# A conv feed-forward in two phases: the up projection first, its products in DRAM, then a down projection that accumulates its whole contraction in PSUM

## The chip, the core and the metric

The kernel runs on one core of a Trainium2 chip. A core has a matrix engine (TensorE, "PE" in the profile, with its weight loads as "PEld"), a vector engine (DVE), a scalar engine (ACT), a third elementwise engine (POOL) and a sync engine (SP). Each takes its own instructions in the order of its own queue; semaphores make one engine wait for another. Matrix products land in PSUM, which is used here as eight banks of 128 x 512 float32 values; everything else is worked on in SBUF. DMA transfers between SBUF and DRAM are issued from the queues of SP, POOL or ACT.

The metric is the device time of one execution in microseconds (us), lower is better.

## The reference, cut to what matters

One decoder layer (512 tokens, model width 2048) is computed: a modulated norm, two attention mixers, an output projection with residual, and then the feed-forward, which alone is changed here:

```python
D_MODEL, SEQ, D_FF, CONV_W = 2048, 512, 5632, 3

def conv_ffn(h, w_up, w_conv, b_conv, w_down):
    S = h.shape[1]
    u = h @ w_up                                   # (512, 2048) @ (2048, 11264)
    up = jnp.pad(u, ((0, 0), (CONV_W - 1, 0), (0, 0)))
    conv = b_conv
    for j in range(CONV_W):
        conv = conv + w_conv[j] * up[:, j:j + S]
    gate, val = jnp.split(conv, 2, axis=-1)
    return (jax.nn.silu(gate) * val) @ w_down      # (512, 5632) @ (5632, 2048)

h = rms_norm(x, g_ffn[l]) * (1.0 + sc_f) + sh_f
x = x + gt_f * conv_ffn(h, w_up[l], w_conv[l], b_conv[l], w_down[l])
```

All inputs and the output are float32.

## The kernel before

**Products of float32.** Every large product is made from three passes. A float32 operand is split into a high part (rounded by ACT to the type float32r) and a low remainder (DVE: operand minus high part). `mm3` (line 120) then issues three matmuls into the same bank: high x high, high x low, low x high (lines 121, 122, 123). `split` (line 116) does this for an activation tile of 128 x 512.

**Storage.** SBUF has 75 equal slots of 128 x 512 (`get`, `getr` for the type float32r, `put` to give back), handed out first in, first out. Weights go through `wtile` (line 97): SP loads 128 x 1024 values into one of five raw buffers, ACT makes the high part (line 110) in one of three buffers, DVE the remainder (line 111) in one of three. `wtile` runs at raised priority, so the scheduler puts the weights of later steps ahead of other work in the queues of SP, ACT and DVE.

**Who decides the order.** The program text is not the order of the queues: a scheduler with its own estimate of durations places the instructions of each engine; buffers and data dependences bind it.

**Up projection.** `lin_fm` (line 125) computes four 128-row tiles of the transposed result: stationary operand the weights, moving operand the activations `h2` (16 pairs of slots, high and low). One step takes two of the 16 tiles of the contraction and issues 24 matmuls into four banks. A block of 512 columns is eight steps.

**The loop.** `NG` = 11 groups of 512 feed-forward columns. Each group (lines 1126 to 1162) runs one up block for the gate columns and one for the value columns, on alternate halves of the PSUM banks (`half`, line 155). `conv` (line 1083) takes a finished bank through one ACT pass with bias and scale (line 1085) and two DVE passes that add the shifted rows (lines 1086, 1087). The gate tile goes through SiLU on ACT; `ev_v` multiplies value by gate (line 1144), splits the product and keeps the four pairs as `fs`.

**Down projection.** `down` (line 1093) runs one group behind: after the up blocks of a group the previous group's `fs` is multiplied with its 512 rows of `w_down`, for four blocks of 512 output columns. `lin_tm` (line 140) does this: stationary operand the activations, moving operand the weights, two contraction tiles a step, four token tiles in four banks, so that each bank takes six matmuls in a row. The sum over the 11 groups is kept in 16 SBUF slots `acc_f`: group 0 copies the banks there (ACT, line 1108), groups 1 to 9 add them (DVE, line 1118), and for group 10 the accumulators are first multiplied by the gate row `gf` (line 1101) and added to the residual `x1`, loaded from DRAM (lines 1100, 1102); each bank is then multiplied by `gf` (line 1113), added to that (line 1114) and stored by SP (line 1115).

**Beside it.** The rest of the adaLN modulation is computed in the gaps of the up blocks: a `ticker` calls `ada_stream` once in four steps, which loads 512 KB into a raw buffer and runs two DVE operations (lines 721, 723). `flush_cols` (line 747) sums such a block through two matmuls into a bank (lines 752, 753), and DVE adds a bias (line 757) that POOL has loaded (line 756).

Of the kernel before, what the change touches and what calls it, by code (L numbers as in the profile page):

```python
# [10 lines left out]
F32 = mybir.dt.float32  # L11
# [3 lines left out]
AF = mybir.ActivationFunctionType  # L15
ALU = mybir.AluOpType
AX = mybir.AxisListType

P = 128
T = 512  # L20
# [11 lines left out]
def trunk_layer_kernel(  # L32
# [28 lines left out]

# [1 line left out]
    cur = [None] * n_slots  # L63
# [3 lines left out]
    def get(dt=F32):  # L67
        i = free.popleft()
        if cur[i] is None or cur[i].dtype != dt:
            cur[i] = pool.tile([P, T], dt, name=f"slot{i}", tag=f"slot{i}")  # L70
        held[id(cur[i])] = i
        return cur[i]

    def getr():
        return get(F32R)

    def put(*ts):
        for t in ts:
            free.append(held.pop(id(t)))
# [36 lines left out]
    def split(dst_hi, dst_lo, src):  # L116
        A.activation(dst_hi, src, AF.Copy)  # L117
        V.tensor_tensor(dst_lo, src, r32(dst_hi), ALU.subtract)

    def mm3(o, lh, ll, rh, rl, first, last):  # L120
        PE.matmul(o, lh, rh, start=first, stop=False)  # L121
        PE.matmul(o, lh, rl, start=False, stop=False)  # L122
        PE.matmul(o, ll, rh, start=False, stop=last)  # L123
# [16 lines left out]
    def lin_tm(src, c0, n, act, K, banks, evac, k0=0, tick=None):  # L140
        for kg in range(0, K, 2):
            wh, wl = wtile(src, k0 + kg, 2, c0, n)
            for tb in range(4):
                ts = slice(tb * P, (tb + 1) * P)
                for i in range(2):
                    k = kg + i
                    ah, al = act[k]
                    mm3(banks[tb][:, :n], ah[:, ts], al[:, ts], wh[:, i, :], wl[:, i, :],
                        k == 0, k == K - 1)
                if kg + 2 == K:  # L150
                    evac(tb, banks[tb][:, :n])
            if tick:
                tick()

    def half():
        cnt["half"] += 1
        return bank[4:8] if cnt["half"] % 2 == 0 else bank[0:4]

# [1 line left out]
    ident = pool.tile([P, P], F32, name="ident")  # L160
# [49 lines left out]
    A.activation(c_act, bank[7][:, 0:16], AF.Silu)  # L210
    # causal bias: zeros, then the triangle of the diagonal block
    zslot = get()
# [9 lines left out]

# [1 line left out]
    ssx = pool.tile([P, 16], F32, name="ssx")  # L224
# [41 lines left out]

# [1 line left out]
    mod = pool.tile([P, 96], F32, name="mod")  # L268
# [43 lines left out]

    # input projection in quarters of the contraction: A = indexer, B = sparse k/v and part of the gates
    part = {"A": [get() for _ in range(7)], "B": [get() for _ in range(7)]}
# [101 lines left out]

# [1 line left out]
    pos_f = gslot[0:4, 384:384 + P]  # L418
# [77 lines left out]

# [1 line left out]
    kit = part["A"][6]  # L498
# [77 lines left out]

# [1 line left out]
    sq = [get(), get()]  # L578
# [51 lines left out]

# [1 line left out]
    att = {}  # L632
# [71 lines left out]

# [1 line left out]
    ada_blocks = [8, 9, 10, 11, 16, 17, 18, 19, 12, 13, 14, 15, 20, 21, 22, 23]  # L706
# [68 lines left out]

# [1 line left out]
    gate_d = [dram.tile([P, T], F32, name=f"gate{k}") for k in range(2 * KD)]  # L777
# [21 lines left out]

# [1 line left out]
    krot = pool.tile([P, 4, 64], F32, name="krot")  # L801
# [42 lines left out]

# [1 line left out]
    pairs = {}  # L846
# [96 lines left out]

    # first branch projection, kept in DRAM
    pa_d = [dram.tile([P, T], F32, name=f"pa{k}") for k in range(KD)]
# [28 lines left out]

# [1 line left out]
    ob = reload(ob_d) + [tuple(att["o"][0:2]), tuple(att["o"][2:4])]  # L976
# [34 lines left out]

# [1 line left out]
    ss1 = pool.tile([P, 16], F32, name="ss1x")  # L1013
# [66 lines left out]

# [1 line left out]

# [6 lines left out]

    acc_f = [[None] * 4 for _ in range(4)]  # L1090
    gf = []

    def down(grp, fs):
        last = grp == NG - 1
        for db in range(4):
            if last:
                for tb in range(4):
                    t = acc_f[tb][db]
                    xt = get()
                    G.dma_start(xt, x1_d[db][tb])  # L1100
                    V.tensor_tensor(t, t, gf[db], ALU.mult)
                    V.tensor_tensor(t, t, xt, ALU.add)
                    put(xt)

            def ev(tb, b, db=db):
                if grp == 0:
                    acc_f[tb][db] = t = get()
                    A.activation(t, b, AF.Copy)
                    return
                t = acc_f[tb][db]  # L1110
                if last:
                    o = get()
                    V.tensor_tensor(o, b, gf[db], ALU.mult)  # L1113
                    V.tensor_tensor(o, o, t, ALU.add)  # L1114
                    SP.dma_start(out[tb * P:(tb + 1) * P, db * 512:(db + 1) * 512], o)
                    put(o)
                else:
                    V.tensor_tensor(t, t, b, ALU.add)  # L1118

            lin_tm(w_down, db * 512, 512, fs, 4, half(), ev, k0=grp * 4)  # L1120
        for t in fs:
            put(*t)

    prev = None
    NG = DFF // 512
    for grp in range(NG):
        gt = []
        if grp == NG - 2:
            while next(stream, 0) is None:
                pass  # L1130

        def ev_g(m, b, grp=grp):
            t = conv(grp * 4 + m, b)
            A.activation(t, t, AF.Silu)
            gt.append(t)

        bk = half()
        flush_cols(bk[3])
        lin_fm(w_up, grp * 512, h2, KD, bk, ev_g, tick=ticker(TF))
        fs = []  # L1140

        def ev_v(m, b, grp=grp):
            t = conv(44 + grp * 4 + m, b)
            V.tensor_tensor(t, t, gt[m], ALU.mult)
            hi, lo = getr(), getr()
            split(hi, lo, t)
            put(t, gt[m])
            fs.append((hi, lo))

        bk = half()  # L1150
        flush_cols(bk[3])
        lin_fm(w_up, DFF + grp * 512, h2, KD, bk, ev_v, tick=ticker(TF))
        if grp == NG - 1:
            for t in h2:
                put(*t)
            put(*ada_acc)
            for db in range(4):
                gf.append(get())
                G.dma_start(gf[db], gtr_d[20 + db])
        if prev is not None:  # L1160
            down(*prev)
        prev = (grp, fs)
    down(*prev)

# [25 lines left out]
```

## Time and profile before

| | us |
|---|---|
| median of 3 runs | 2795.78 (2795.48 to 2797.96) |
| span of the profiled execution, first to last instruction | 2791.8 |
| TensorE busy in it | 2753.4 |
| start of the first up matmul (L121) | 1314.29 |
| start of the last down matmul (L123) | 2786.91 |
| end of the last DVE operation | 2788.75 |

How to read the profile's rows: a busy row gives the busy time of each engine, its share of the span and the number of instructions. A window row gives the stretch in us, its length, and then, for PE, PEld, DVE, ACT and POOL, busy us and the number of instructions; at its end stand the granted TensorE clock (1.00 is full), the busy share of the 16 DMA engines and GB/s. A group row gives line, engine, operation, output <- inputs, shape and count, then busy us and mean ns of one, then the engine's idle time before these instructions and what ended it. A timeline row gives start, duration, engine, line and operation; in brackets the idle time before it. A DMA row gives the count, the size of one and the median time from issue to landing. Matmuls are pipelined: one lasts about 0.39 us, but the next starts 0.23 us after it.

### The profile page before, as it was taken

What the parts mean: (1) busy time and instruction counts of PE and PEld (TensorE: products, weight loads), DVE (VectorE), ACT (ScalarE), POOL (GpSimd) and SP (SyncE); (2) the same over time, 40 slices, a digit from 0 to 9 for tenths busy, and PEclk for the clock granted to TensorE, in tenths of its full rate; (3) what the DMA queues carried; (4) which work ended last, traced back from release to release, by engine and by line L of the source; (5) the groups of instructions that cost most, each with busy time, mean ns of one, the idle gap of its engine ahead of it and who ended that gap; (6) DMA issues with size and microseconds to landing.
All of it is one profiled execution on the core that took longest, in us unless ns stands there. A gap on an engine that the chain in (4) does not pass through costs nothing.

```text
span 2791.8 us, 31818 instructions
## 1 busy us (share of the span) xinstructions
PE 2753.4 (99%) x12160; PEld 2204.5 (79%) x12160; DVE 1550.7 (56%) x2615; ACT 903.2 (32%) x1309; POOL 177.5 (6%) x355
## 2 busy tenths in 40 slices
PE   6999999999999999999999999999999999999999
PEld 5877777788887768887888888888888888888887
DVE  7987975544467658546444353635263544434357
ACT  4333433322344553224333222222223231313231
POOL 1000100100031231000000000000000000000010
PEclk8999999999999999999999999999999999999999
DMA  9942245655464587645333433334343333333352
GB/s 321 362 138 87 68 138 176 203 188 174 151 204 132 161 293 255 207 153 186 91 98 103 123 106 113 121 106 122 98 129 98 114 98 99 97 92 98 97 168 98
DMA packets 222604, 409.43 MB, mean 147 GB/s; under 512 B 16714, under 2 KB 58084, under 8 KB 222452
## 3 DMA queue, kind: packets, MB, share of 16 engines
q1 hardware_dynamic: 200628, 348.59, 40.0%
q0 software_dynamic: 21792, 58.81, 6.2%
q8 instruction: 95, 1.56, 0.2%
q14 instruction: 57, 0.47, 0.1%
q10 hardware_dynamic: 32, 0.01, 0.0%
HBM read 376.93 MB, written 30.41 MB: 146 GB/s over the span
## 4 chain that ended last, share of the span: by engine, by line
PE 53%; DVE 0%; ACT 0%; issue 0%
PE bank L121 18%; PE bank L123 17%; PE bank L122 17%; DVE slot L1114 0%; DVE slot L1113 0%; PE bank L240 0%; ACT slot L1043 0%; PE bank L752 0%; PE bank L753 0%; ACT slot L1075 0%; PE bank L1041 0%
## 5 line engine op out<-in xcount | busy, mean ns | idle before, releaser
L111 DVE TENSOR_TENSOR wlo<-raw,whi 128x1024 fp32r<-128x1024 f32 (+2 forms) x462 | 558.2, 1209 | 868.6 <-ACT whi L110 865.6
L110 ACT ACTIVATE whi<-raw 128x1024 fp32r<-128x1024 f32 (+2 forms) x462 | 483.8, 1049 | 1418.4 <-PE bank L122 755.7
L121 PE MATMUL bank<-slot,whi 128*128 128x512 f32 (+1 forms) x2192 | 868.4, 398 | 2.7 <-ACT slot L1075 1.5
L122 PE MATMUL bank<-slot,whi 128*128 128x512 f32 (+1 forms) x2192 | 866.3, 395 | 0.0
L123 PE MATMUL bank<-slot,wlo 128*128 128x512 f32 (+1 forms) x2192 | 861.7, 396 | 0.0
L121 PE MATMUL bank<-whi,slot 128*128 128x512 f32 (+2 forms) x1472 | 572.1, 392 | 7.2 <-ACT slot L384 6.5
L122 PE MATMUL bank<-wlo,slot 128*128 128x512 f32 (+2 forms) x1472 | 575.6, 391 | 0.0
L123 PE MATMUL bank<-whi,slot 128*128 128x512 f32 (+2 forms) x1472 | 566.1, 389 | 0.0
L123 PEld LDWEIGHTS bank<-slot,wlo 128*128 128x128 f32 (+1 forms) x2192 | 411.0, 188 | 99.4 <-issue 1.9
L121 PEld LDWEIGHTS bank<-slot,whi 128*128 128x128 f32 (+1 forms) x2192 | 410.7, 187 | 98.7 <-ACT whi L110 2.1
L122 PEld LDWEIGHTS bank<-slot,whi 128*128 128x128 f32 (+1 forms) x2192 | 411.1, 188 | 96.8 <-issue 1.3
L121 PEld LDWEIGHTS bank<-whi,slot 128*128 128x128 f32 x1472 | 278.1, 189 | 71.4 <-ACT slot L384 6.7
L122 PEld LDWEIGHTS bank<-wlo,slot 128*128 128x128 f32 x1472 | 278.2, 189 | 59.2 <-issue 0.2
L123 PEld LDWEIGHTS bank<-whi,slot 128*128 128x128 f32 x1472 | 276.9, 188 | 60.7 <-issue 0.9
L723 DVE SCALAR_TENSOR_TENSOR slot<-raw,c_act,slot 128x512 f32<-128x512 f32 x240 | 179.9, 749 | 175.8 <-DMA raw<-in_w_ada 172.8
L1118 DVE TENSOR_TENSOR slot<-slot,bank 128x512 f32<-128x512 f32 x144 | 95.3, 681 | 22.8 <-PE bank L123 22.6
L298 DVE SCALAR_TENSOR_TENSOR slot<-slot,c_act,slot 128x512 f32<-128x512 f32 x110 | 78.7, 746 | 5.7 <-DMA slot<-in_w_ada 5.0
L1085 ACT ACTIVATE slot<-bank,wcv 128x512 f32<-128x512 f32 x88 | 68.0, 773 | 32.6 <-PE bank L123 32.6
L117 ACT ACTIVATE slot<-slot 128x512 fp32r<-128x512 f32 x76 | 47.3, 624 | 78.3 <-DVE slot L998 28.0
L1086 DVE SCALAR_TENSOR_TENSOR slot<-bank,wcv,slot 128x511 f32<-128x511 f32 x88 | 65.5, 744 | 3.8 <-ACT slot L1085 1.3
L1087 DVE SCALAR_TENSOR_TENSOR slot<-bank,wcv,slot 128x510 f32<-128x510 f32 x88 | 65.6, 746 | 1.9
L756 POOL DMA_DIRECT2D slot<-in_b_ada x8 | 4.4, 551 | 911.5 <-ACT whi L110 865.9
(252 smaller groups left out, 1594.8 us busy)
## 6 DMA issues: line engine op xcount, KB each, us to landing
raw<-in_w_up SPq DMA_DIRECT2D x176, 512.0 KB, 3.7
raw<-in_w_ada SPq DMA_DIRECT2D x128, 512.0 KB, 3.9
raw<-in_w_down SPq DMA_DIRECT2D x88, 512.0 KB, 3.6
raw<-in_w_in SPq DMA_DIRECT2D x82, 512.0 KB, 3.7
slot<-in_w_ada SPq DMA_DIRECT2D x128, 256.0 KB, 6.0
raw<-in_w_o SPq DMA_DIRECT2D x32, 512.0 KB, 4.7
raw<-in_w_in SPq DMA_DIRECT2D x16, 552.0 KB, 6.9
gate<-slot POOLq DMA_DIRECT2D x32, 256.0 KB, 3.8
```

The source lines that it names most:

```text
L110: A.activation(hi, raw[:, :w], AF.Copy)
L111: V.tensor_tensor(lo, raw[:, :w], r32(hi), ALU.subtract)
L117: A.activation(dst_hi, src, AF.Copy)
L121: PE.matmul(o, lh, rh, start=first, stop=False)
L122: PE.matmul(o, lh, rl, start=False, stop=False)
L123: PE.matmul(o, ll, rh, start=False, stop=last)
L298: stt[g] = V.scalar_tensor_tensor(acc, raw, c_act[:, k:k + 1], acc, op0=ALU.mult, op1=ALU.add)
L723: V.scalar_tensor_tensor(acc, t[:, i], c_act[:, k:k + 1], acc, op0=ALU.mult, op1=ALU.add)
L1085: A.activation(t, b, AF.Identity, bias=wcv[:, 3, j:j + 1], scale=wcv[:, 2, j:j + 1])
L1086: V.scalar_tensor_tensor(t[:, 1:], b[:, :T - 1], wcv[:, 1, j:j + 1], t[:, 1:], op0=ALU.mult, op1=ALU.add)
L1087: V.scalar_tensor_tensor(t[:, 2:], b[:, :T - 2], wcv[:, 0, j:j + 1], t[:, 2:], op0=ALU.mult, op1=ALU.add)
L1118: V.tensor_tensor(t, t, b, ALU.add)
```

## The change

The eleven groups no longer alternate. `up_group` runs the two up blocks of a group as before, but writes each product `f` (128 x 512, float32) to a DRAM buffer of its own, `f_d[j]`, from POOL's queue; there are 44. After all groups, `h2` is given back, and all 44 products are loaded into 44 slots (`fr`) from POOL's queue, with the four gate rows `gf`. The down projection then goes over the output columns in two halves (`c2`). For each half it goes once over all 44 contraction tiles: a step loads 128 rows x 1024 columns of `w_down`, splits the product `fr[k]` (so each product is split once for each half), and issues 3 matmuls into each of the eight banks, 24 in all. The sum over the contraction stays in PSUM; the accumulators `acc_f`, their copies, adds, scaling and residual passes are gone. With the last contraction tile each bank is multiplied by `gf`, the residual, loaded by POOL, is added, and SP stores the result. Section comments were also removed.

```diff
-    acc_f = [[None] * 4 for _ in range(4)]
-    gf = []
-
-    def down(grp, fs):
...
-    prev = None
+    NF_ = DFF // P
     NG = DFF // 512
+    f_d = [dram.tile([P, T], F32, name=f"f{j}") for j in range(NF_)]
+
+    def up_group(grp):
+        gt = []
+
+        def ev_g(m, b):
+            t = conv(grp * 4 + m, b)
+            A.activation(t, t, AF.Silu)
+            gt.append(t)
+
+        bk = half()
+        flush_cols(bk[3])
+        lin_fm(w_up, grp * 512, h2, KD, bk, ev_g, tick=ticker(TF))
+
+        def ev_v(m, b):
+            t = conv(44 + grp * 4 + m, b)
+            V.tensor_tensor(t, t, gt[m], ALU.mult)
+            G.dma_start(f_d[grp * 4 + m], t)
+            put(t, gt[m])
+
+        bk = half()
+        flush_cols(bk[3])
+        lin_fm(w_up, DFF + grp * 512, h2, KD, bk, ev_v, tick=ticker(TF))
+
     for grp in range(NG):
-        gt = []
         if grp == NG - 2:
             while next(stream, 0) is None:
                 pass
...
-            hi, lo = getr(), getr()
-            split(hi, lo, t)
-            put(t, gt[m])
-            fs.append((hi, lo))
...
-        if prev is not None:
-            down(*prev)
-        prev = (grp, fs)
-    down(*prev)
+        up_group(grp)
+    for t in h2:
+        put(*t)
+    put(*ada_acc)
+
+
+    fr = []
+    for j in range(NF_):
+        t = get()
+        G.dma_start(t, f_d[j])
+        fr.append(t)
+    gf = [get() for _ in range(4)]
+    for db in range(4):
+        G.dma_start(gf[db], gtr_d[20 + db])
+    for c2 in range(2):
+        for k in range(NF_):
+            wh, wl = wtile(w_down, k, 1, c2 * 1024, 1024)
+            fh, fl = getr(), getr()
+            split(fh, fl, fr[k])
+            for cb in range(2):
+                ns = slice(cb * 512, (cb + 1) * 512)
+                for tb in range(4):
+                    ts = slice(tb * P, (tb + 1) * P)
+                    mm3(bank[cb * 4 + tb], fh[:, ts], fl[:, ts], wh[:, 0, ns], wl[:, 0, ns], k == 0, k == NF_ - 1)
+                    if k == NF_ - 1:
+                        db = c2 * 2 + cb
+                        xt, o = get(), get()
+                        G.dma_start(xt, x1_d[db][tb])
+                        V.tensor_tensor(o, bank[cb * 4 + tb], gf[db], ALU.mult)
+                        V.tensor_tensor(o, o, xt, ALU.add)
+                        SP.dma_start(out[tb * P:(tb + 1) * P, db * 512:(db + 1) * 512], o)
+                        put(xt, o)
+            put(fh, fl)
```

More of the change, by code (lines that the diff above doesn't have):

```diff
@@ L1088, in conv @@
         return t
-    acc_f = [[None] * 4 for _ in range(4)]
-    gf = []
-    def down(grp, fs):
[L1094 to L1122, printed above, removed]
-    prev = None
+    NF_ = DFF // P
     NG = DFF // 512
-    for grp in range(NG):
+    f_d = [dram.tile([P, T], F32, name=f"f{j}") for j in range(NF_)]
+    def up_group(grp):
         gt = []
[L1128 to L1132, printed above, removed]
+        def ev_g(m, b):
             t = conv(grp * 4 + m, b)
@@ L1139, in trunk_layer_kernel @@
         lin_fm(w_up, grp * 512, h2, KD, bk, ev_g, tick=ticker(TF))
-        fs = []
-        def ev_v(m, b, grp=grp):
+        def ev_v(m, b):
             t = conv(44 + grp * 4 + m, b)
             V.tensor_tensor(t, t, gt[m], ALU.mult)
-            hi, lo = getr(), getr()
-            split(hi, lo, t)
+            G.dma_start(f_d[grp * 4 + m], t)
             put(t, gt[m])
-            fs.append((hi, lo))
         bk = half()
@@ L1152, in trunk_layer_kernel @@
         lin_fm(w_up, DFF + grp * 512, h2, KD, bk, ev_v, tick=ticker(TF))
[L1153 to L1159, printed above, removed]
-        if prev is not None:
-            down(*prev)
-        prev = (grp, fs)
-    down(*prev)
+    for grp in range(NG):
+        if grp == NG - 2:
+            while next(stream, 0) is None:
+                pass
+        up_group(grp)
[29 more added lines that the diff above has]
+            put(fh, fl)
 _INS = ['x', 'c', 'positions', 'g_attn', 'g_ffn', 'w_ada', 'b_ada', 'w_in', 'g_qa', 'g_ka', 'g_mq_lat',
```

## The prediction

> **What bounds the kernel now.** I read the page's busy line first, then the same busy times for two stretches of the feed-forward, then the list of what TensorE waited for, then the last microseconds in order of time.
>
> ```profile
> PE 2753.4 (99%) x12160; PEld 2204.5 (79%) x12160; DVE 1550.7 (56%) x2615; ACT 903.2 (32%) x1309; POOL 177.5 (6%) x355
> 1334.00:2780.00 1446.00, 1446.00 (x6231) 1169.41 (x6230) 653.89 (x784) 402.23 (x458) 15.06 (x28) 1.00 0.35 108
> 2716.00:2780.00 64.00, 64.00 (x277) 51.72 (x276) 50.15 (x72) 10.62 (x10) 0.00 (x0) 1.00 0.29 103
> PE bank L121 <- ACT slot L1075: 1.5, 1, 1.5
> ```
>
> The columns of the two middle rows are busy time and count of PE, PEld, DVE, ACT and POOL, then the granted clock, the DMA share and GB/s. From 1334 to 2780 us TensorE is busy 1446.00 of 1446.00 us at clock 1.00. It starts one matmul every 1446/6231 = 0.232 us; in the last 64 us, where only the down projection runs, every 64/277 = 0.231 us. Up and down therefore have the same pace, and in both the clock is full. The last row is the last wait of any length that stands against a feed-forward matmul: 1.5 us on the first operand, before the stretch. DVE is busy 45% of it and ACT 28%. So this phase is worth its matmul count times 0.232 us, and a change can only move what happens where TensorE must wait, and what follows its last matmul:
>
> ```profile
> 2782.73 0.39 PE L123 MATMUL bank<-whi,slot 128*128 128x512 f32 x1
> 2783.16 0.69 DVE L1113 TENSOR_TENSOR slot<-bank,slot 128x512 f32<-128x512 f32 x1 [5.08 <-PE bank L123]
> 2783.88 0.69 DVE L1114 TENSOR_TENSOR slot<-slot,slot 128x512 f32<-128x512 f32 x1
> 2784.55 0.69 DVE L1113 TENSOR_TENSOR slot<-bank,slot 128x512 f32<-128x512 f32 x1
> ...
> 2786.91 0.39 PE L123 MATMUL bank<-whi,slot 128*128 128x512 f32 x1
> 2787.34 0.69 DVE L1113 TENSOR_TENSOR slot<-bank,slot 128x512 f32<-128x512 f32 x1
> 2788.06 0.69 DVE L1114 TENSOR_TENSOR slot<-slot,slot 128x512 f32<-128x512 f32 x1
> ```
>
> The last matmul of a bank starts, 0.43 us later DVE multiplies that bank, then adds. A bank takes six matmuls (1.39 us) and its two DVE operations take 1.39 us too (2783.16 to 2784.55), so DVE keeps up: the last add ends at 2788.75, 1.84 us after the start of the last matmul. The span ends 2791.8 - 2788.75 = 3.05 us later, with the last store.
>
> **The change, part by part.** *TensorE:* nothing is removed or added. Up keeps 22 x 8 x 24 = 4224 matmuls, down keeps 44 x 16 x 3 = 2112, and the built program has as many instructions on this engine as before. 0 us, if it still never waits.
>
> *DVE and ACT:*
>
> ```profile
> L111 DVE TENSOR_TENSOR wlo<-raw,whi 128x1024 fp32r<-128x1024 f32 x258 | 315.6, 1223 | 712.0 <-ACT whi L110 711.7
> L1118 DVE TENSOR_TENSOR slot<-slot,bank 128x512 f32<-128x512 f32 x144 | 95.3, 681 | 22.8 <-PE bank L123 22.6
> L1087 DVE SCALAR_TENSOR_TENSOR slot<-bank,wcv,slot 128x510 f32<-128x510 f32 x88 | 65.6, 746 | 1.9
> L1086 DVE SCALAR_TENSOR_TENSOR slot<-bank,wcv,slot 128x511 f32<-128x511 f32 x88 | 65.5, 744 | 3.8 <-ACT slot L1085 1.3
> L723 DVE SCALAR_TENSOR_TENSOR slot<-raw,c_act,slot 128x512 f32<-128x512 f32 x44 | 33.0, 750 | 42.8 <-DMA raw<-in_w_ada 42.4
> L118 DVE TENSOR_TENSOR slot<-slot,slot 128x512 fp32r<-128x512 f32 x48 | 32.7, 682 | 1.8 <-ACT slot L117 1.7
> L1144 DVE TENSOR_TENSOR slot<-slot,slot 128x512 f32<-128x512 f32 x44 | 30.0, 682 | 0.0
> L1101 DVE TENSOR_TENSOR slot<-slot,slot 128x512 f32<-128x512 f32 x16 | 10.8, 684 | 0.0
> L1102 DVE TENSOR_TENSOR slot<-slot,slot 128x512 f32<-128x512 f32 x16 | 10.7, 684 | 0.0
> L110 ACT ACTIVATE whi<-raw 128x1024 fp32r<-128x1024 f32 x258 | 273.5, 1060 | 952.2 <-PE bank L122 617.3 <-PE bank L123 292.2 <-issue 42.6
> L1085 ACT ACTIVATE slot<-bank,wcv 128x512 f32<-128x512 f32 x88 | 68.0, 773 | 32.6 <-PE bank L123 32.6
> L117 ACT ACTIVATE slot<-slot 128x512 fp32r<-128x512 f32 x48 | 29.7, 621 | 25.8 <-DVE slot L1144 21.1 <-DVE slot L723 4.7
> L1108 ACT ACTIVATE slot<-bank 128x512 f32<-128x512 f32 x16 | 9.5, 594 | 7.2 <-PE bank L123 7.2
> ```
>
> Gone are the 144 accumulator adds (95.3 us) and the 32 operations on the accumulators in the last group (21.5); each f is split twice instead of once, 44 x 0.682 = 30.0 more. DVE is relieved by about 87 us. ACT loses 16 copies (9.5) and gains 44 x 0.621 = 27.3. Neither engine held TensorE up, so this is worth 0. The cover: an up group now runs 16 x 24 x 0.232 = 89.1 us alone, and DVE's share of it is 16 x 1.223 + 8 x (0.744 + 0.746) + 4 x 0.682 + 8 x 0.750 (the adaLN stream) = 40.2 us; a down step lasts 24 x 0.232 = 5.57 us, with 1.22 + 0.68 us of DVE and 1.06 + 0.62 of ACT. Without that cover a step would cost its late operand's 1 to 2 us.
>
> *POOL and DMA:*
>
> ```profile
> raw<-in_w_down SPq DMA_DIRECT2D x88, 512.0 KB, 3.6
> gate<-slot POOLq DMA_DIRECT2D x32, 256.0 KB, 3.8
> slot<-gate POOLq DMA_DIRECT2D x32, 256.0 KB, 5.3
> slot<-x POOLq DMA_DIRECT2D x16, 256.0 KB, 3.0
> 2780.00:2792.00 12.00, 7.30 (x32) 5.58 (x30) 5.46 (x8) 0.00 (x0) 0.00 (x0) 0.89 0.23 87
> ```
>
> POOL gets 44 stores and 44 loads of 256 KB; f makes the same trip as the branch gates, 3.8 us out and 5.3 back. 23 MB over 1446 us is 16 GB/s beside 108, at a DMA share of 0.35. In the built order the load of f0 stands right behind the store of f24, and the loads up to f32 stand before the last group's stores f40 to f43; what is loaded behind these is wanted from step 33 on, 33 x 5.57 = 184 us later. Down weights keep 512 KB and 3.6 us. 0 us.
>
> *First handover, up to down.* Time 0 is the end of the last up matmul. The splits for the first six steps and the weights of the first two stand in ACT's and DVE's queues ahead of the last group's convolution. Banks 0 to 3 have been free for 44 us; banks 4 to 7 each need an ACT pass and two DVE passes. Walking both queues in the built order with the durations above, the four banks are free at -1.5, 0.7, 6.0 and 8.1 us. TensorE's queue puts matmuls of steps 1 and 2 between those of step 0 and comes to banks 4 to 7 after 13, 22, 44 and 53 matmuls: 3.0, 5.1, 10.2 and 12.3 us. Over 4 us are left each time: 0. Behind the waiting matmul stand all later ones, so a late bank would cost its full lateness.
>
> *Second handover, first to second half of the columns.* All eight banks are full at once. Time 0 is the start of the last step of the first half. A bank is finished every 0.70 us; DVE has the eight multiplies, a weight remainder, a split and five adds in between. With 0.69 us for each, the multiplies end at 1.6, 3.5, 4.8, 5.5, 6.9, 8.2, 9.6 and 11.0 us. In the built order TensorE does steps 0 and 1 of the second half bank by bank, so it comes to the banks at 5.6, 7.0, 8.4, 9.7, 11.1, 12.3, 13.7 and 14.9 us. At least 3.5 us are left. The next weight remainders are ready at 12.9 and 19.9 us, wanted at 16.7 and 23.9. From step 5 on some of ACT's splits go into slots that an output store must leave first (3.05 us after its add); this is counted in the 19.9. 0 us.
>
> *The end.* Now a bank ends after three matmuls, 0.70 us, and DVE's two operations cannot keep up. Their spacing decides:
>
> ```profile
> 2773.46 0.68 DVE L1113 TENSOR_TENSOR slot<-bank,slot 128x512 f32<-128x512 f32 x1
> 2774.05 1.28 DVE L1114 TENSOR_TENSOR slot<-slot,slot 128x512 f32<-128x512 f32 x2
> 2775.26 0.68 DVE L1113 TENSOR_TENSOR slot<-bank,slot 128x512 f32<-128x512 f32 x1
> ```
>
> Operations that don't need the one just ahead start 0.60 us apart (2773.46, 2774.05, 2775.26: 1.80 for three); an add right behind its own multiply gives 0.70 a piece (2783.16 to 2784.55). In the built order no add stands right behind its own multiply, so I take 0.60. Let E be the start of the last matmul. Bank 0's last matmul starts 21 x 0.2325 = 4.88 earlier, its multiply at E - 4.45, bank 1's at E - 3.75; 14 more operations at 0.60 put the last start at E + 4.65 and its end at E + 5.34. Before it was E + 1.84: **+3.5 us**, and +4.9 with 0.70. A store takes all 16 DMA engines 12 x 0.23 / 4 = 0.69 us; the last three now follow 0.60 apart, so the last lands 0.2 later (bounds 0 and one whole store, 0.7).
>
> Sum: 2791.8 + 3.5 + 0.2 = 2795.5 us of span. The median of the runs lies 2795.78 - 2791.8 = 4.0 above the span, so **2799.5 us**, 0.13% more. The bound of 0.2%, about what a measurement of this kernel can tell from no change, is 5.6 us: 2801.4.
>
> **Rivals.**
> *A, slower: the second handover blocks.* All eight banks must be emptied by DVE while TensorE wants them back. It decides from where DVE falls 3.5 us behind my walk: if the adds, waiting for their residual loads, hold the multiplies behind them. Then 16 operations of 0.69 us (11.0) stand against 5.6 us of matmuls, and TensorE loses up to 5.4: 2804.9. For it: only DVE empties banks here. Against: the residual loads take 3.0 us and are issued into slots free 30 us earlier.
> *B, slower: the trip through DRAM comes onto the path* at the first handover, or POOL's queue holds loads behind a late store. The price is ACT 0.77, DVE 0.74 + 0.75 + 0.68, store 3.8, load 5.3, split 1.3: 13.3 us, 2812.8. Against: the loads' place in the queue, two groups ahead.
> *C, slower: the clock drops, since banks now change every three matmuls.*
>
> ```profile
> 0.00:100.00 100.00, 75.33 (x369) 64.10 (x370) 74.86 (x134) 42.03 (x75) 11.31 (x78) 0.90 1.01 332
> 1319.97 1.10 PE L121 MATMUL bank<-slot,whi 128*128 128x512 f32 x4
> ```
>
> The only low clock here, 0.90, belongs to a stretch where TensorE is idle a quarter of the time. At 0.90 the 2112 down matmuls, 490 us, would take 54 longer: 2853. Four matmuls in a row into four banks (1319.97) show no gap, so little speaks for it. The Trainium skill (TensorE: Matmul & The Clock Gate, "A second HAM failure mode: psum-queue depth-cycling") tells of a kernel that cycled through PSUM banks each iteration and let its clock oscillate; by that rule this change would pay. The trace does not bear it out: the old down projection changes banks too, at clock 1.00.
> *D, faster:* only if the matmuls quicken, since all that follows the last one's start is 4.9 us. To gain 5.6 us beyond the longer tail, the 2112 down matmuls would have to start (5.6 + 3.7)/2112 = 4.4 ns closer, about 2790. The rows spread by 1 ns, and the pace is the same with DVE at 78% (50.15 of 64.00) as at 45%.
>
> **How the numbers follow.** Forecast 0.63, A 0.16, B 0.13, C 0.03, D 0.05. Slower by over 0.2% is A, B and C, 0.32; faster is D, 0.05; within is 0.63. The likeliest case's own range is 2799 to 2801.4 (tail 3.5 to 4.9, stores 0 to 0.7). The range 2797 to 2806 leaves out B, C and most of D, 0.2.
>
> **What would show it.** Right: TensorE busy all the time from the first up matmul to the last down matmul, no wait on a bank at either handover, the last add ending 5.3 us after the start of the last matmul, 16 closing operations 0.60 apart. Wrong: a wait of a down matmul for a DVE slot or bank near the middle of the down phase (A), for ACT's split with a DMA behind it (B), a clock under 1.00 there (C), or a matmul pace other than 0.232 us.

## The result and the profile after

Over 18 runs of each on one chip the changed kernel took 2800.97 us (median, 2798.75 to 2806.43) and the kernel before 2795.62 (2792.65 to 2800.73). The ratio is 1.002, 95% interval [1.0013, 1.0027]: some 3.6 to 7.5 us more, against the forecast of 2799.5. The bound of 0.2% lies inside that interval. The profiled execution has a span of 2798.2 us.

The page's busy line of the changed kernel, then its rows by window (the same stretches as before), then its DMA issues of f:

```profile
PE 2752.1 (98%) x12160; PEld 2202.4 (79%) x12160; DVE 1475.0 (53%) x2483; ACT 917.2 (33%) x1337; POOL 226.0 (8%) x443
```

```profile
1334.00:2780.00 1446.00, 1446.00 (x6230) 1169.32 (x6229) 574.85 (x643) 418.03 (x489) 61.66 (x115) 1.00 0.40 123
2716.00:2780.00 64.00, 64.00 (x277) 51.72 (x277) 14.17 (x12) 11.66 (x11) 4.29 (x8) 1.00 0.29 88
```

```profile
f<-slot POOLq DMA_DIRECT2D x44, 256.0 KB, 3.0
slot<-f POOLq DMA_DIRECT2D x44, 256.0 KB, 4.6
```

The matmuls did what they did before: 6230 in the long stretch where there were 6231, busy 1446.00 of 1446.00 us, clock 1.00. DVE's share of that stretch fell from 653.89 to 574.85 us and nothing came of it. Both handovers lie inside the stretch, and the list of TensorE's waits is empty from 1330 us to the end, so no bank was waited for at either. The trip of f through DRAM took 3.0 us out and 4.6 back.

The end, in order of time:

```profile
2785.24 1.39 DVE L1148 TENSOR_TENSOR slot<-bank,slot 128x512 f32<-128x512 f32 x2 [9.54 <-PE bank L123]
2786.54 0.68 DVE L1149 TENSOR_TENSOR slot<-slot,slot 128x512 f32<-128x512 f32 x1
2787.14 0.69 DVE L1148 TENSOR_TENSOR slot<-bank,slot 128x512 f32<-128x512 f32 x1
...
2789.70 0.39 PE L123 MATMUL bank<-whi,slot 128*128 128x512 f32 x1
...
2793.14 1.88 DVE L1149 TENSOR_TENSOR slot<-slot,slot 128x512 f32<-128x512 f32 x3
```

DVE starts an operation every 0.60 us (2786.54, 2787.14), falls behind the banks, and ends at 2793.14 + 1.88 = 2795.02, 5.32 us after the start of the last matmul.

The spans differ by 6.4 us, but they must not be compared as they are. The first transpose of the second norm (line 1041), which lies ahead of the change, starts at 1302.04 in the profile of before and at 1303.38 here; over the twelve profiles of this study it starts between 1299.88 and 1308.17, with the same instructions ahead of it. So I count from that transpose and cut the rest at three events: the first up matmul, the start of the last down matmul, the end of the last DVE operation. All values in us, read off the timelines; a span is given to 0.1 us, so the last two columns are good to about 0.05. Each ratio is against runs of the kernel before that were taken beside it.

| kernel | ratio of times, 95% interval | entry | up and down | tail | store | sum |
|---|---|---|---|---|---|---|
| before | 1 | 12.25 | 1472.62 | 1.84 | 3.05 | 1489.76 |
| after | 1.002 [1.0013, 1.0027] | 12.99 | 1473.33 | 5.32 | 3.18 | 1494.82 |
| e1_tail | 1.0003 [0.9995, 1.0012] | 12.98 | 1473.34 | 2.26 | 3.04 | 1491.62 |
| e2_entry | 1.0017 [1.0009, 1.0026] | 12.16 | 1472.78 | 5.32 | 3.18 | 1493.44 |
| e3_both | 1.0003 [0.9994, 1.0011] | 11.93 | 1472.79 | 2.26 | 3.00 | 1489.98 |
| e4_gate_in_weights | 1.0105 [1.0082, 1.0128] | 12.49 | 1498.29 | 1.11 | 3.05 | 1514.94 |
| e5_double_trip | 1.0012 [1.0002, 1.0021] | 13.04 | 1473.33 | 5.33 | 3.15 | 1494.85 |
| e6_triple_multiply | 1.0026 [1.0015, 1.0036] | 12.53 | 1477.81 | 5.32 | 3.19 | 1498.85 |
| e8_quarters | 1.0002 [0.9993, 1.0011] | 12.82 | 1473.41 | 1.85 | 3.02 | 1491.10 |
| e9_loads_behind_stores | 1.006 [1.0044, 1.0076] | 12.61 | 1485.64 | 5.32 | 3.20 | 1506.77 |
| e10_gate_held_back | 1.0001 [0.9992, 1.001] | 12.98 | 1474.91 | 1.12 | 3.02 | 1492.03 |
| e11_gate_held_entry | 0.9994 [0.9985, 1.0003] | 12.52 | 1472.83 | 1.11 | 3.07 | 1489.53 |

The changed kernel is 5.06 us longer by this count: 3.48 in the tail, 0.13 in the store, 0.74 at the entry and 0.71 after the first up matmul. The last two, 1.45 us, had no place in the prediction, and a part of them is chance. Here is what TensorE waited for from 1290 to 1330 us, first in the kernel before, then in the changed one (us in total, times, longest):

```profile
PE bank L121 <- ACT slot L1075: 1.5, 1, 1.5
PE bank L752 <- ACT slot L1043: 0.7, 1, 0.7
PE bank L1041 <- ACT slot L1043: 0.4, 1, 0.4
```

```profile
PE bank L121 <- ACT slot L1075: 1.4, 1, 1.4
PE bank L752 <- ACT slot L1043: 1.1, 1, 1.1
PE bank L1041 <- ACT slot L1043: 0.8, 2, 0.4
PE bank L122 <- DVE slot L1076: 0.3, 1, 0.3
```

The wait of line 752 grew by 0.4, a second wait of 0.4 stands at line 1041, both for ACT's copies of the transposes (line 1043), and a new wait stands on the first `h2` remainder (line 1076).

The first of these is chance. The copy that line 752 waits for stands on ACT behind work that waits for DVE's residual adds (line 1031), and DVE itself had waited for the landing of an adaLN weight, first in the kernel before, then in the changed one:

```profile
1296.90 1.54 DVE L723 SCALAR_TENSOR_TENSOR slot<-raw,c_act,slot 128x512 f32<-128x512 f32 x2 [2.78 <-DMA raw<-in_w_ada]
```

```profile
1298.61 1.54 DVE L723 SCALAR_TENSOR_TENSOR slot<-raw,c_act,slot 128x512 f32<-128x512 f32 x2 [2.72 <-DMA raw<-in_w_ada]
```

That is 5.14 us ahead of the first transpose (1302.04) in the one and 4.77 ahead of it (1303.38) in the other. The order up to there is the same in all twelve profiles, yet the wait of line 752 lies between 0.44 and 1.17 us. Taken off the entry, it leaves 11.49 to 11.50 us in the four profiles with the old order behind the transposes (before, e2, e3, e11) and 11.87 to 11.88 in the eight with the changed kernel's. So of the 0.74 at the entry 0.38 belongs to the change and 0.37 is chance.

The timeline of the changed kernel tells where the rest comes from:

```profile
1310.03 0.63 ACT L1043 ACTIVATE slot<-bank 128x512 f32<-128x512 f32 x1
1310.50 0.68 ACT L117 ACTIVATE slot<-slot 128x512 fp32r<-128x512 f32 x1
...
1311.02 2.59 ACT L1043 ACTIVATE slot<-bank 128x512 f32<-128x512 f32 x5
...
1315.76 0.69 DVE L118 TENSOR_TENSOR slot<-slot,slot 128x512 fp32r<-128x512 f32 x1
1316.36 0.75 DVE L723 SCALAR_TENSOR_TENSOR slot<-raw,c_act,slot 128x512 f32<-128x512 f32 x1
...
1317.03 0.75 DVE L1076 SCALAR_TENSOR_TENSOR slot<-slot,mod,slot 128x512 fp32r<-128x512 f32 x1
1317.83 0.19 PEld L122 LDWEIGHTS bank<-slot,whi 128*128 128x128 f32 x1 [0.69 <-DVE slot L1076]
```

ACT splits a finished adaLN block (line 117) between two copies, 0.68 us; DVE does the other half of that split and a step of the next block (lines 118 and 723) right ahead of the remainder of `h2` for which TensorE waits. The fifth up matmul (line 122) starts 1.46 us after the first one (1316.37); in the kernel before it was 1.04. In the kernel before none of these three stands there. The diff does not touch them; that the scheduler placed them earlier because other work stands behind them is argued, not shown.

### The profile page after: what moved, and what is told of

The parts are those of the page before. It is cut to its first block, busy times and chain, and to the rows that moved or that the text cites. A ratio compares the mean times of both kernels' runs of the same rounds, so it can differ in the third digit from the quotient of the medians.

```text
span 2798.2 us, 31958 instructions
## 1 busy us (share of the span) xinstructions
PE 2752.1 (98%) x12160; PEld 2202.4 (79%) x12160; DVE 1475.0 (53%) x2483; ACT 917.2 (33%) x1337; POOL 226.0 (8%) x443
## 4 chain that ended last, share of the span: by engine, by line
PE 76%; issue 13%; DMA 5%; DVE 3%; POOL 1%; ACT 0%; SPq 0%; POOLq 0%; DVEq 0%; ACTq 0%
PE bank L121 25%; PE bank L122 24%; PE bank L123 24%; DMA raw<-in_w_ada 3%; DMA slot<-in_w_ada 1%; DVE wlo L111 1%; DVE slot L723 1%; DMA raw<-in_w_in 1%; PE bank L934 1%; PE bank L677 0%; POOL x L1033 0%; POOL slot L1025 0%; DMA slot<-gate 0%; DMA pa<-slot 0%; DMA slot<-in_x 0%
## 5 line engine op out<-in xcount | busy, mean ns | idle before, releaser
L118 DVE TENSOR_TENSOR slot<-slot,slot 128x512 fp32r<-128x512 f32 x120 | 82.1, 688 | 206.0 <-PE bank L122 191.0
L117 ACT ACTIVATE slot<-slot 128x512 fp32r<-128x512 f32 x120 | 74.2, 621 | 61.9 <-DVE slot L998 22.0
L1109 POOL DMA_DIRECT2D f<-slot x44 | 23.8, 542 | 735.9 <-DVE slot L1108 735.7
```

## The experiments

**The tail (e1).** The last two contraction steps of the second half are done bank by bank, so that each of the closing banks takes six matmuls in a row again.

```diff
-        for k in range(NF_):
...
+        for k0 in list(range(NF_ - 2)) + [NF_ - 2] if c2 else range(NF_):
+            ks = (k0, k0 + 1) if c2 and k0 == NF_ - 2 else (k0,)
```

> The last two steps of the second half are merged bank by bank, so that a bank closes every six matmuls (1.39 us) instead of three; nothing else is changed. Theory (the loss is the tail, 3.5 us, and a reshuffled entry, 1.5 us): the last add ends 1.8 us after the start of the last matmul instead of 5.3; the entry stays; the time falls by 3.5 us against the changed kernel, to about +1.5 us (0.05%) against the kernel before. Rival (second handover or the trip through DRAM holds TensorE up in a way the list of waits hides): the time stays at about +5.3 us, whatever the tail does.

Measured: a tail of 2.26 us in place of 5.32, the entry as in the changed kernel, a ratio of 1.0003. The last closing operations, in order of time, with the last matmul's start at 2786.20:

```profile
2785.24 0.69 DVE L1153 TENSOR_TENSOR slot<-bank,slot 128x512 f32<-128x512 f32 x1 [0.36 <-PE bank L123]
2785.85 1.28 DVE L1154 TENSOR_TENSOR slot<-slot,slot 128x512 f32<-128x512 f32 x2
2787.05 0.68 DVE L1153 TENSOR_TENSOR slot<-bank,slot 128x512 f32<-128x512 f32 x1
2787.77 0.69 DVE L1154 TENSOR_TENSOR slot<-slot,slot 128x512 f32<-128x512 f32 x1
```

DVE waits for a bank again before two of its operations (0.36 us here), so it is no longer the bound all along. The last multiply stands behind two adds and starts 0.85 us after the last matmul where 0.43 was walked, so the tail is 0.4 longer than expected. Nothing else was touched: 3.1 us of the loss are the tail.

**The entry (e2).** The adaLN split is held behind the last pair of `h2`, and so are the operations of the next block.

```diff
+        with tc.issue_after(lo_i[-1].ins), tc.issue_after(hi_i[-1].ins):
+            flush_cols(b)
...
+            with tc.issue_after(lo_i[-1].ins) if done[0] > 12 else nullcontext():
+                base()
```

> Only the order at the entry is put back: the split of a finished adaLN block and the DVE operations of the next one are queued behind the last h2 pair, as they stood in the kernel before. Theory: the first up matmul starts 12.2 us after the first transpose of the second norm, as before the change, instead of 13.0, and its 0.26 us wait for L1076's result is gone; 1.0 to 1.5 us less than the changed kernel; the tail stays at 5.3. Rival (entry differences are scatter of one execution): the interval from the first transpose stays near 13.0, or moves without reference to the order.

Measured: entry 12.16 (12.25 before the change), up and down 1472.78, together 1.38 us less than in the changed kernel. Of this 0.45 is the chance wait of line 752 (1.12 there, 0.67 here), as the rival had it; the order is worth the other 0.93, 0.38 at the entry and 0.55 behind it. Line 1041 waits only once, as before the change, and line 122 no more:

```profile
PE bank L752 <- ACT slot L1043: 0.7, 1, 0.7
PE bank L1041 <- ACT slot L1043: 0.4, 1, 0.4
```

The ratio, 1.0017 with an interval 0.0017 wide, can't tell 0.9 us; the trace carries this verdict.

**Both (e3).** The two edits together.

> Both edits of the two kernels before. Theory: equal to the kernel before within 0.5 us (ratio 1.0000, 0.9998 to 1.0003); first up matmul to last down matmul 1472.6 us, as before. Rivals: what is left above the kernel before is what the two phases cost by themselves; the handover or the DRAM trip would leave 2 us or more.

Measured: 1489.98 from the first transpose to the end, 0.22 us more than the kernel before, ratio 1.0003 [0.9994, 1.0011]. The chance wait of line 752 was short here, 0.44 us against 0.75; without it the difference is 0.53: 0.42 in the tail and 0.17 in up and down, less 0.05 in the store. So the tail and the order at the entry are the loss, but for half a microsecond.

**Quarters (e8).** Two phases and the DRAM trip stay; the down projection takes 512 columns at a time into four banks, two contraction tiles a step.

```diff
-    for c2 in range(2):
-        for k in range(NF_):
-            wh, wl = wtile(w_down, k, 1, c2 * 1024, 1024)
+    for db in range(4):
+        bk = half()
+        for kg in range(0, NF_, 2):
+            wh, wl = wtile(w_down, kg, 2, db * 512, 512)
```

> Two phases and the trip through DRAM stay, but the down projection goes over the columns in four quarters of 512, two contraction tiles a step into four banks, alternating halves of PSUM; each product is split four times, not twice. A bank now closes every six matmuls (1.39 us), as in the kernel before. My theory: the last add ends 1.8 us after the start of the last matmul (5.3 in the changed kernel), so 3.5 us less, about 2797.5; no bank is waited for at a handover, since the next quarter has the other four. The 88 splits more (0.62 us of ACT and 0.68 of DVE each) stay hidden. Rival: the splits or the loads of the weights are late with the two-tile step and TensorE loses more than the 3.5.

Measured: tail 1.85, entry as changed, up and down 1473.41; 3.7 us less than the changed kernel. The 88 splits more cost nothing. That bears out the tail by a second way: what decides is how many matmuls a bank gets before it closes.

**The trip through DRAM, doubled (e5).**

```diff
+            G.dma_start(f2_d[grp * 4 + m], t)
...
+        G.dma_start(t, f2_d[j])
```

> The trip of f through DRAM is doubled: each product is stored to two DRAM buffers and loaded from both, one after the other, into the same slot (88 stores and 88 loads of 256 KB in place of 44 and 44). My theory: the trip is hidden behind the matmuls, so the stretch from the first up matmul to the start of the last down matmul stays at 1473.3 us (at most 0.5 more) and the time stays that of the changed kernel, about 2801 us. Rival B (the trip is on the path, at least in part): the second store and load behind the first add up to 3.8 + 5.3 us at the first handover, and TensorE waits there for ACT's or DVE's split.

Measured: up and down 1473.33, the same to the hundredth, and the sum 1494.85 against 1494.82. Rival B had no part in it.

**The trip, uncovered (e9).** All 44 loads are held behind the last store.

```diff
+        with tc.issue_after(st[-1].ins):
+            G.dma_start(t, f_d[j])
```

> All 44 loads of f are held in POOL's queue behind the last of the 44 stores, so that the trip through DRAM stands openly at the handover from up to down. By the price of rival B (ACT 0.77, DVE 0.74 + 0.75 + 0.68, store 3.8, load 5.3, split 1.3: 13.3 us from the last up matmul to the first operand) TensorE waits about 13 us there, and the time is about 2814. If the wait is under 5 us, the rival's price was too high and the place of the loads in the queue did not matter much; if much over 13, the 44 loads bunched together cost more than one trip.

Measured: up and down 1485.64, 12.3 us longer. What TensorE waited for, the split that released it, the last store and the first loads on POOL's queue, and two windows behind the wait:

```profile
PE bank L121 <- ACT slot L117: 10.4, 1, 10.4
```

```profile
2311.61 0.63 ACT L117 ACTIVATE slot<-slot 128x512 fp32r<-128x512 f32 x1 [8.21 <-DMA slot<-f]
```

```profile
2307.99 0.54 POOL L1111 DMA_DIRECT2D f<-slot  x1 [0.85 <-DVE slot L1110]
2308.52 6.35 POOL L1132 DMA_DIRECT2D slot<-f  x12
```

```profile
2312.30:2315.90 3.60, 3.60 (x9) 2.83 (x10) 3.33 (x5) 3.15 (x5) 3.37 (x7) 0.50 1.02 371
2316.00:2320.00 4.00, 4.00 (x19) 3.21 (x18) 2.61 (x4) 2.07 (x4) 2.12 (x5) 1.00 0.99 381
```

10.4 us are the wait for f's load. Most of the rest is the clock: for 3.6 us after the wait it stood at 0.50, and 9 matmuls started where 15.5 fit (3.60/0.232): 6.5 x 0.232 = 1.5 us. So it is the place of the loads in POOL's queue that keeps the trip off the path. That the total is near rival B's 13.3 is luck, because the wait is made of other parts: the last up matmul starts at 2301.47, the last of four stores is issued at 2307.99, since the four products follow one another through DVE, and the first load, of a product stored long before, takes 3.1 us (2308.52 to 2311.61). No store's landing is in it; the price had one chain of 2.9 us, a store of 3.8 and a load of 5.3.

**The second handover, loaded (e6).** There, and only there, each bank is multiplied three times.

```diff
-                        V.tensor_tensor(o, bank[cb * 4 + tb], gf[db], ALU.mult)
+                        for _ in range(1 if c2 else 3):
+                            V.tensor_tensor(o, bank[cb * 4 + tb], gf[db], ALU.mult)
```

> At the handover between the two halves of the columns each bank is multiplied by its gate row three times into the same slot in place of once: 16 more DVE operations of 0.6 to 0.7 us, 9.6 to 11 us, none at the end of the kernel. The prediction walked 3.5 us of slack there. If that walk is right, TensorE now waits there for banks about 6 to 7.5 us in all, and the time is about 2807 us; fewer than 3 us would mean that the slack was larger than walked, and 9 us or more that there was none, so that rival A was close to deciding.

Measured: up and down 4.48 us longer, less than expected. The wait, and DVE's queue at that place:

```profile
PE bank L121 <- DVE slot L1149: 3.5, 3, 1.6
```

```profile
2543.13 1.22 DVE L111 TENSOR_TENSOR wlo<-raw,whi 128x1024 fp32r<-128x1024 f32 x1
2544.26 8.46 DVE L1149 TENSOR_TENSOR slot<-bank,slot 128x512 f32<-128x512 f32 x14
2552.63 1.22 DVE L111 TENSOR_TENSOR wlo<-raw,whi 128x1024 fp32r<-128x1024 f32 x1
```

Fourteen multiplies take 8.46 us, 0.60 apart. The sixteen more are 9.6 us, and 4.5 came through. The difference of 5.1 is not the slack of the changed kernel, though: the first add stands only at 2553.76 here, behind 15 multiplies, while in the changed kernel the adds stand between the multiplies, and six of the 24 multiplies start after TensorE's last wait (2555.70) and cost it nothing. The slack is read from the changed kernel itself, the multiplies of the handover against TensorE's return to the banks:

```profile
2539.91 0.69 DVE L1148 TENSOR_TENSOR slot<-bank,slot 128x512 f32<-128x512 f32 x1 [0.17 <-PE bank L123]
...
2541.66 0.68 DVE L1148 TENSOR_TENSOR slot<-bank,slot 128x512 f32<-128x512 f32 x1
...
2546.00 0.40 PE L121 MATMUL bank<-whi,slot 128*128 128x512 f32 x1
...
2548.25 0.68 DVE L1148 TENSOR_TENSOR slot<-bank,slot 128x512 f32<-128x512 f32 x1
```

The last step of the first half starts at 2539.02, and TensorE begins the second half at 2544.61, by the built order with six matmuls a bank. The second multiply ends at 2542.34 and TensorE comes to the second bank at 2546.00: 3.7 us are left there, the least of all; the walk had 3.5, at the same bank. For the last bank it had too little: its multiply ends at 2548.93, 9.9 us after the start of the step, where the walk, with 0.69 an operation in place of 0.60, had 11.0.

**The gate row in the weights, a miss (e4).** To halve the closing work, the down weights are multiplied by the gate row before they are split (two DVE operations on each raw buffer), and each bank closes with one add.

```diff
+            SP.dma_start(raw[:, :1024], src[k0 * P:(k0 + 1) * P, c0:c0 + 1024])
+            for j in range(2):
+                r = raw[:, j * 512:(j + 1) * 512]
+                V.tensor_tensor(r, r, gs[j], ALU.mult)
...
-                        V.tensor_tensor(o, bank[cb * 4 + tb], gf[db], ALU.mult)
-                        V.tensor_tensor(o, o, xt, ALU.add)
+                        V.tensor_tensor(o, xt, bank[cb * 4 + tb], ALU.add)
```

> The changed kernel, but the gate row is multiplied into the down weights before they are split, not into the result; two more DVE operations a step (88 x 2 x 0.60 = 106 us, under a step of 5.57), and one DVE operation a bank at the end instead of two. TensorE's order at the end stays as in the changed kernel. Theory (DVE cannot close banks as fast as they come): one operation of 0.60 keeps up with 0.70, the last add ends 0.43 + 0.69 = 1.1 us after the start of the last matmul, the time falls by 4.2 us to about +1.2 us. Rival (the three matmuls a bank, or the stores that bunch up, make the tail): it stays at 4 us or more.

Measured: the tail came out at 1.11 us, but up and down took 1498.29, 25.0 us more. DVE's timeline in the down phase (line 125 is the multiply, 127 the remainder):

```profile
2491.11 1.29 DVE L125 TENSOR_TENSOR raw<-raw,slot 128x512 f32<-128x512 f32 x2 [3.71 <-DMA raw<-in_w_down]
2492.33 1.22 DVE L127 TENSOR_TENSOR wlo<-raw,whi 128x1024 fp32r<-128x1024 f32 x1
2497.92 1.29 DVE L125 TENSOR_TENSOR raw<-raw,slot 128x512 f32<-128x512 f32 x2 [4.37 <-DMA raw<-in_w_down]
2499.13 1.22 DVE L127 TENSOR_TENSOR wlo<-raw,whi 128x1024 fp32r<-128x1024 f32 x1
2503.90 1.29 DVE L125 TENSOR_TENSOR raw<-raw,slot 128x512 f32<-128x512 f32 x2 [3.55 <-DMA raw<-in_w_down]
```

In the built order the multiply of a raw buffer stands right behind the remainder that frees the same buffer. DVE works in order, so remainder, load and multiply form a chain: 6.8 us from the multiply at 2491.11 to the next, then 6.0, where a step of matmuls lasts 5.57. Everything else on DVE, the handover's adds among it, stands behind it. TensorE's listed waits come to 9.9 us for a remainder (15 times) and 5.7 for a bank at the handover. The waits for a remainder fall late in each half (the first ones at 2481.49 and 2694.67); why the chain kept pace before isn't shown. Behind the longest waits the clock fell as well, here after one of 1.76 us:

```profile
2770.70:2774.30 3.60, 3.55 (x9) 2.77 (x10) 0.16 (x1) 0.00 (x0) 0.00 (x0) 0.54 0.54 193
```

What else makes up the 25 us was not resolved.

**The miss, mended (e10).** The multiply is held behind the remainder of the weight three before.

```diff
+                with tc.issue_after(lo_w[-3].ins) if len(lo_w) > 4 else nullcontext():
+                    V.tensor_tensor(r, r, gs[j], ALU.mult)
```

> As e4_gate_in_weights, but the multiply of a weight by the gate row is held behind the remainder of the weight three before it, so that on DVE's queue it no longer stands right behind the remainder that frees its own raw buffer. My theory of that miss: remainder (1.22), load (some 3.5) and multiply (1.29) of one raw buffer stood in a chain of 6.0 us per step against 5.57 us of matmuls; with two remainders between, the load has two steps more, DVE no longer waits for a landing, TensorE loses nothing from the first up matmul to the last, 1473 us, and with a tail of 1.1 us the span's end comes 4 us earlier than in the changed kernel: about 2796 to 2797. Rival: DVE's 1.29 us per step itself is too much (52% busy in the first miss), or the closing adds stand behind the multiplies at the handover; then most of the 16 us stay, and the time is over 2810.

Measured: the waits for the landing are gone (line 130 is the remainder now, 128 the multiply):

```profile
2490.90 1.23 DVE L130 TENSOR_TENSOR wlo<-raw,whi 128x1024 fp32r<-128x1024 f32 x1 [3.08 <-ACT whi L129]
2492.04 1.28 DVE L128 TENSOR_TENSOR raw<-raw,slot 128x512 f32<-128x512 f32 x2
2496.47 1.23 DVE L130 TENSOR_TENSOR wlo<-raw,whi 128x1024 fp32r<-128x1024 f32 x1 [3.14 <-ACT whi L129]
```

The step is 5.57 us again (2490.90 to 2496.47) and the ratio 1.0001. So the 25 us came from the order on DVE, not from its load: its operations are the same. Up and down took 1474.91, 1.6 us over the changed kernel, all of it in the first 10 us:

```profile
1321.15:1331.15 10.00, 9.74 (x34) 7.49 (x35) 9.88 (x16) 5.01 (x7) 0.60 (x1) 0.83 0.28 80
```

The clock stood at 0.83 there and 34 matmuls started; in the changed kernel it was 41 at 1.00. The 7 missing ones are 1.6 us.

**The same, with the entry put back (e11).**

> The kernel with the multiply held back, and with the adaLN split and the next block's operations behind the last pair of h2 (as in e2_entry). If the terms add up, entry 12.1, 1472.8 from first up matmul to the last down matmul, tail 1.1, store 3.05: 1489.1 against 1489.8 in the kernel before, so the same time as before, at best 0.7 us less; no version of this change that keeps the count of matmuls can be more than some 5 us faster, since TensorE is busy all the time between.

Measured: 1489.53, of which the entry was 12.52, 0.4 longer than expected; the chance wait among the transposes (line 769 here) was 1.03 us (0.67 in e2), and without it the entry is 11.49, as in e2. Ratio 0.9994 [0.9985, 1.0003]. The interval still holds 1, so this version isn't shown to beat the kernel before.

## Why the prediction was right, and where it was not

- **Matmul count and pace, 0 us:** right. 6230 matmuls in the same 1446 us, no wait in it.
- **DVE and ACT, 0 us:** right. DVE lost 79 us of work in that stretch (75.7 in the whole span by the busy lines, where the sum had 87) and TensorE gained nothing. Quarters gave ACT and DVE 88 splits more, and that too changed nothing.
- **The trip through DRAM, 0 us:** right, and shown from both sides: doubled it cost nothing, uncovered 12.3 us. Rival B's price came near that by luck: the wait is made of other parts.
- **First handover, 0 us:** right by the trace (no wait). The last convolution pass of banks 4 to 7 (line 1087) ends at 2297.62, 2299.54, 2304.38 and 2306.30; with the walk's count of matmuls TensorE comes to them at 2302.26, 2304.36, 2309.48 and 2311.59. At least 4.6 us were left, where the walk had over 4. No run tried to use them up.
- **Second handover, 0 us:** right, with 3.7 us of slack at the least, where the walk had 3.5. Rival A was as far off as thought. The run that loaded this handover (e6) was forecast at 6 to 7.5 us of waiting and lost 4.5, and a part of the added work stood behind TensorE's last wait.
- **The end, +3.5:** right, 3.48 by the traces (5.32 against 5.34 forecast), with the 0.60 spacing as chosen and not 0.70. Two different edits take it away, e1 down to 2.26 and e8 to 1.85.
- **The stores, +0.2:** 0.13.
- **Clock (rival C) and rival D:** the granted clock is 1.00 and the pace 0.231 to 0.232 us. The rule of the Trainium skill (TensorE: Matmul & The Clock Gate, "A second HAM failure mode: psum-queue depth-cycling") tells of a kernel whose matrix engine is idle for short times between its groups of matmuls. On neither side of the change is there such idle time here (1446.00 of 1446.00 us busy), so a low clock did not come, and what the rule would do with such gaps is not tested. The prediction called 0.90 the only low clock of the kernel before; its own row 2780:2792 has 0.89, and 200 to 300 us has 0.97. Neither lies in the stretch that the argument rests on.
- **What was left out:** the order at the entry, 0.93 us (0.38 ahead of the first up matmul, 0.55 behind it; e2 takes both away). The prediction quoted the very row, 1.5 us on the first operand "before the stretch", said that a change can only move what happens where TensorE must wait, and then costed no such place ahead of the feed-forward. The built order would have shown the three moved instructions; it was walked at the handovers and the end alone.

The 5.06 us between the two traces are then 3.61 for the tail and the stores, which the prediction had at 3.7, 0.93 for the order at the entry, 0.37 of chance at line 752, and 0.16 in up and down for which no wait shows. Between the medians it is 5.35, with an interval of 3.6 to 7.5 that can't tell these terms apart. The forecast came out 1.5 us low. That the likeliest case's own range, 2799 to 2801.4, still held 2800.97 is in part luck: its upper end allowed for a spacing of 0.70 that did not come, and this made room for the step left out. The bound of 0.2% (5.6 us) was all but reached.

Not settled: why the time of the same instructions up to 1302 us differs by up to 8 us from one execution to the next, and where the last 0.16 us come from.

## What to carry to other kernels

Where one engine was busy all the time at full clock, relief for the others was worth nothing here; cost the few places where it can wait: the entry, each handover, the tail. A contraction kept whole in all eight banks, with three matmuls a bank in its last step, let the banks close faster (every 0.70 us) than two DVE operations could empty them (1.20 us), and this was paid at the end: finish the last steps bank by bank, so that the closing rate matches the emptying rate. When a diff changes the work behind a stretch, compare the order ahead of it too, and put an instruction that waits for a load behind the work that doesn't. Before a small difference between two single profiles is put down to a change, look for a wait in it whose cause lies ahead of the change.

## What the runs showed of the hardware that was not expected

- After a wait of 10.4 us TensorE ran 3.6 us at a granted clock of 0.50 (e9), so the idle gap cost 1.5 to 2 us more than its length. The Trainium skill (TensorE: Matmul & The Clock Gate, "What's actually happening") states a clock that falls to half after an idle window of about 3.4 us and comes back after about as long of work; that trace agrees, while the two falls of the next point came without so long a wait. The three waits of up to 1.6 us in e6 left the clock of their window (25 us from 2540 on) at 1.00.
- At the entry, where the longest wait is 1.4 us, one profile of twelve showed the clock at 0.83 over 10 us (e10), at a cost of 1.6 us; the others show 1.00. In e4 the clock was 0.54 for 3.6 us behind a wait of 1.76 us. So it fell behind waits much shorter than in e9, and behind others of about the same length it did not; it was not tried what decides it.
- Fourteen DVE multiplies from PSUM in a row took 8.46 us (e6): 0.60 us apart, like the mix of multiplies and adds in the tail. That they read PSUM, and that the three of a bank write the same slot, didn't slow them.
